# Fixing the order of all engines in the joints into the even and the odd layer, with the norms split into steps between the products

## Chip, cores and metric

One core of one Trainium2 chip. The time is that of the whole program on the device, in microseconds (us), as a median of runs.

## What is computed

Two blocks, one after the other, on 1024 rows of 1024 features. The first is a transformer layer with experts; the second has an even and an odd layer. The places of this change are where the even layer begins (behind the experts' scatter) and where the odd layer begins (behind the even layer's output projection). Both begin with a row norm and a large projection:

```python
def rmsnorm_2(x, g):
    xf = x.astype(jnp.float32)
    y = xf * lax.rsqrt(jnp.mean(xf * xf, axis=-1, keepdims=True) + EPS)
    return (y * g.astype(jnp.float32)).astype(x.dtype)

def even_layer(x, norm_g, w_in, pool_w, pool_scale, ws, bs, w_out):
    h = rmsnorm_2(x, norm_g)
    z = h @ w_in
    ...
    return x + jnp.concatenate([y_a, y_b], axis=-1) @ w_out

def odd_layer(x, norm_g, w_in, conv_w, w_out):
    h = rmsnorm_2(x, norm_g)
    z = h @ w_in
    ...
```

## The kernel before

Rows of x are handled as eight token tiles of 128; tiles t and t + 4 form a pair, so there are four pairs, t = 0 to 3. The projections run as seven products of half-size matrices instead of eight (B11, T2, T1, T3, B21, T4, B22; `unit`, L1212 to L1266), each matmul on a high and a low part of its operands, 12 matmuls a product. They need sums of the halves of the weight and of the normed, transposed x.

`norm_pair` makes those of x for one pair. It squares both tiles on ScalarE (ACT, L230), forms 1/rms with small steps on VectorE (DVE) and one root on ACT (`rstd`, L176 to L182), multiplies the first tile by 1/rms and the norm's row on DVE (L1283) and the second on ACT (L1284) and GpSimd (POOL, L1285), transposes four blocks on TensorE (PE, L1291), and writes seven operands with a high part (cast on ACT, L1297) and a low part (DVE L136 or POOL L134), with differences on DVE (L1302 to L1310). Called with a `high_priority` hint, it is woven by the scheduler into what stands around it. The squares' output that nobody reads (`junk`) takes a buffer of the tag pq, of which there are two, as for the unit's p1, q and r.

`operands` is a generator that loads weight quarters (`raw`), forms the four sums S (L1182, L1183, L1187, L1192) on DVE and splits each operand (`split`: cast L1166 on ACT, low part L134 on POOL). `feed` draws the first seven operands of a stage.

`unit` runs seven products into three banks a, b, c of the tag mm: p1 = B11 is copied by ACT (L1242), q = p1 + T2 on DVE (L1245), r = q + T3 on DVE (L1251), and the results leave through `put` (L1262 copy on ACT, L1264 sum on DVE). T2, T3 and T4 go through the same bank b. With `sub` it does one half of the columns, 256 wide: the first half needs the pairs t = 0 and 1, the second (`sub` = 1) t = 2 and 3. So a stage begins: norms of t0 and t1, half unit 0, norms of t2 and t3, half unit 1, then units 512 wide.

**Joint into the even layer** (`even`, first part). Behind the last expert's scatter into xacc on POOL (L1154) the x tiles are loaded (L1402, queue of SyncE, SP), and the row `nrow` (L1397) after the first four of them. Banks for the transposes: s, o, s, o.

**Joint into the odd layer** (end of `even`). The last pass of `out_sums` multiplies the last slice of the even output projection, into two banks of the tag o, and DVE adds each half of a tile to x (the eviction, L1363), in the order of tiles 0, 4, 1, 5, 2, 6, 3, 7; `then` stores each to x3d (L1457) and calls the norm of t0 after tile 5 and of t1 after tile 7. The tags mm and s have three banks, o has two:

```python
self.banks(es, "secp", {"mm": 3, "s": 3, "o": 2})
...
self.out_sums(A["weo"], self.ye, [((15,), (0, 4, 1, 5, 2, 6, 3, 7), then)], ("o",))
self.feed([A["wo7"][i] for i in range(56)], ("X",) * 3)
self.qk = [self.t("qk", [D]) for _ in range(2)]
self.unit(self.put2(self.qk), None, 0)
norm(2)
norm(3)
self.unit(self.put2(self.qk, 0, 1), None, 1)
```

## Time and profile before

| what | value |
|---|---|
| median of 3 runs | 3397.22 us (3395.42 to 3404.03) |
| profiled execution, own time | 3398.43 us |
| its span, first to last instruction | 3396.6 us |
| mean granted TensorE clock | 0.959 |
| TensorE busy | 3097.2 us, 91% |
| DVE, POOL, ACT busy | 2058.0, 1490.8, 1368.6 us |

Times in the rows below are microseconds from the start of the span. An engine's share of busy time is a mean over stages with different limits; the table by stretches shows it stage by stage, and the timeline of one engine shows what each instruction waited for.

### The profile page before, as it was taken

The page shows a single profiled execution, that of the slowest core. Times are in us where ns is not written, and L with a number is a line of the kernel's source. Part 1 is how long each engine was busy: PE and PEld are TensorE (multiplying, and loading weights), DVE is VectorE, ACT ScalarE, POOL GpSimd, SP SyncE. Part 2 cuts the span into 40 slices and gives each one's busy share as a digit, 9 for nine tenths or more (in the row PEclk, how much of TensorE's full clock was granted, in tenths as well). Part 3 has the DMA queues.
Part 4 walks back from the last instruction along what each step waited for, and adds up shares of the span by engine and source line. Part 5 has one row for each costly group of instructions (what it writes and reads, how often), then busy time and mean ns, then how long its engine had stood idle before and what let it go on. Part 6 is the DMA issues. An engine that isn't in the chain of part 4 may idle for free. (4 is left out here: it accounts for less than half of the span.)

```text
span 3396.6 us, 43830 instructions
## 1 busy us (share of the span) xinstructions
PE 3097.2 (91%) x15797; PEld 2559.2 (75%) x15797; DVE 2058.0 (61%) x3793; ACT 1368.6 (40%) x2489; POOL 1490.8 (44%) x1014
## 2 busy tenths in 40 slices
PE   6898888994999679999998899999999999999998
PEld 4787675773777568887786788888888888877787
DVE  5676677776899864555546555555455455444455
ACT  4445345442787643332312434334334333232312
POOL 2443342322233355556563434334334334566673
PEclk8899898897999889999999999999999999999999
DMA  5233321436999512212441111111111111122242
GB/s 195 69 124 101 116 69 42 136 101 238 331 382 375 163 54 75 69 59 75 153 145 66 37 41 53 44 50 47 48 50 46 49 44 50 53 72 68 100 154 75
DMA packets 139710, 358.38 MB, mean 106 GB/s; under 512 B 16946, under 2 KB 26706, under 8 KB 139492
## 3 DMA queue, kind: packets, MB, share of 16 engines
q1 hardware_dynamic: 134596, 337.75, 29.0%
q0 software_dynamic: 4896, 17.83, 2.1%
q8 instruction: 124, 2.03, 0.2%
q14 instruction: 94, 0.77, 0.1%
HBM read 307.23 MB, written 48.28 MB: 105 GB/s over the span
## 5 line engine op out<-in xcount | busy, mean ns | idle before, releaser
L1234 PE MATMUL ps_mm<-h,hi 128*128 128x512 f32 (+1 forms) x4272 | 1089.9, 394 | 41.0 <-DVE pq L1251 10.9
L1234 PEld LDWEIGHTS ps_mm<-h,hi 128*128 128x128 f32 x4272 | 784.0, 189 | 210.9 <-ACT qk L1262 17.2
L134 POOL TENSOR_TENSOR lo<-S,hi 128x512 fp32r<-128x512 f32 x302 | 402.9, 1337 | 600.1 <-PE ps_mm L1234 411.0
L134 POOL TENSOR_TENSOR lo<-raw,hi 128x512 fp32r<-128x512 f32 (+2 forms) x274 | 416.6, 1526 | 345.5 <-ACT hi L1166 219.0
L1234 PE MATMUL ps_mm<-h,lo 128*128 128x512 f32 (+1 forms) x2136 | 566.0, 388 | 0.0
L1234 PEld LDWEIGHTS ps_mm<-h,lo 128*128 128x128 f32 x2136 | 398.9, 189 | 82.5
L1166 ACT CAST hi<-S 128x512 fp32r<-128x512 f32 x302 | 187.0, 620 | 546.4 <-PE ps_mm L1234 530.8
L1166 ACT CAST hi<-raw 128x512 fp32r<-128x512 f32 x240 | 148.9, 622 | 359.4 <-PE ps_mm L1234 308.8
L148 ACT CAST hi<-raw 128x1024 fp32r<-128x1024 f32 (+1 forms) x222 | 230.4, 1048 | 93.1 <-PE ps_mm L162 64.1
L136 DVE TENSOR_TENSOR lo<-raw,hi 128x1024 fp32r<-128x1024 f32 x188 | 247.8, 1347 | 28.2 <-ACT hi L148 25.0
L1187 DVE TENSOR_TENSOR S<-raw,raw 128x512 f32<-128x512 f32 x76 | 66.6, 876 | 190.6 <-POOL lo L134 189.3
L160 PE MATMUL ps_mm<-hi,hxh 128*128 128x256 f32 (+1 forms) x448 | 132.6, 297 | 9.6 <-ACT hxh L364 5.8
L162 PE MATMUL ps_mm<-hi,hxl 128*128 128x256 f32 (+1 forms) x448 | 131.9, 296 | 1.2 <-POOL hxl L134 1.2
L161 PE MATMUL ps_mm<-lo,hxh 128*128 128x256 f32 (+1 forms) x448 | 131.9, 295 | 0.0
L1153 POOL TENSOR_TENSOR y<-y,g 128x1024 f32<-128x1024 f32 x15 | 41.1, 2738 | 197.0 <-ACT y L1149 197.0
L1183 DVE TENSOR_TENSOR S<-S,raw 128x512 f32<-128x512 f32 x76 | 102.8, 1353 | 37.8 <-POOL lo L134 37.3
L161 PE MATMUL ps_mm<-lo,xT 128*128 128x512 f32 x256 | 105.2, 411 | 13.8 <-DVE lo L136 12.5
L1726 DVE CUSTOM_DVE_ANT_0 P<-ps_s,bias 128x128 f32<-128x128 f32 (+1 forms) x192 | 61.8, 348 | 81.4 <-PE ps_s L1721 80.3
L1264 DVE TENSOR_TENSOR qk<-ps_mm,pq 128x512 f32<-128x512 f32 (+1 forms) x75 | 69.1, 938 | 67.5 <-PE ps_mm L1234 67.2
L134 POOL TENSOR_TENSOR yl<-r,yh 128x1024 fp32r<-128x1024 f32 x28 | 68.3, 2440 | 83.8 <-ACT yh L1335 83.8
L160 PE MATMUL ps_mm<-hi,xT 128*128 128x512 f32 x256 | 103.6, 405 | 0.0
L1335 ACT CAST yh<-r 128x1024 fp32r<-128x1024 f32 x28 | 29.4, 1049 | 181.1 <-PE ps_s L161 167.9
(597 smaller groups left out, 6614.8 us busy)
## 6 DMA issues: line engine op xcount, KB each, us to landing
raw<-in_wexp_dram SPq DMA_DIRECT2D x192, 512.0 KB, 8.3
raw<-in_wo_dram SPq DMA_DIRECT2D x228, 256.0 KB, 2.7
raw<-in_we_dram SPq DMA_DIRECT2D x80, 256.0 KB, 2.8
mraw<-in_wmod_dram SPq DMA_DIRECT2D x64, 256.0 KB, 2.7
r<-ye SPq DMA_DIRECT2D x14, 512.0 KB, 4.6
r<-in_weo_dram SPq DMA_DIRECT2D x14, 512.0 KB
r<-yo SPq DMA_DIRECT2D x14, 512.0 KB, 3.6
r<-in_wo_dram SPq DMA_DIRECT2D x14, 512.0 KB
```

Source lines behind the costliest of these rows:

```text
L134: nc.gpsimd.tensor_sub(lo, raw, hi.bitcast(F32))
L136: nc.vector.tensor_sub(lo, raw, hi.bitcast(F32))
L148: self.nc.scalar.copy(hi, raw)
L160: nc.tensor.matmul(out, l[0], r[0], start=start, stop=False)
L161: nc.tensor.matmul(out, l[0], r[1], start=False, stop=False)
L162: nc.tensor.matmul(out, l[1], r[0], start=False, stop=stop)
L1166: self.nc.scalar.copy(hi, x)
L1183: nc.vector.tensor_sub(s2, s1, a11)
L1187: nc.vector.tensor_sub(s3, a11, a21)
L1234: nc.tensor.matmul(ps, w[a][:, kt * P:(kt + 1) * P], h[b][:, kt, cs], start=start and i == 0, stop=i == 11, skip_group_check=True)
L1264: self.nc.vector.tensor_add(dst, ps, add)
L1726: nc.vector.tensor_tensor_reduce(p, ps, bias[:, n - m:], op0=ALU.add, op1=ALU.max, scale=1.0, scalar=-3e38, accum_out=mx[:, j:j + 1])
```

## The change

In both joints the order of the instructions is fixed as the code writes them (`manual_schedule`), on all five engines in the first, on all but SP in the second. `norm_pair` becomes a generator of two pieces: squares, 1/rms and both multiplies, now both on DVE (L1297 after the change); then transposes (L1304) and operands (L1310 to L1323). In the first half unit, `steps` runs the first piece of t3 behind q (after two products), and the second pieces of t2 and t3 behind the sixth and the seventh product; the first piece of t2 stands ahead of the unit. In the pass's `then`, the first pieces of t0 and t1 come behind tiles 4 and 5, the second ones behind tiles 6 and 7. In `feed` the low parts go to POOL and DVE in turn. `nrow` and the first loads of weights are issued ahead of x. New line numbers: eviction L1377, q L1253, r L1260, puts L1275 and L1277, products L1237, x loads L1414.

```diff
--- before.py
+++ after.py
@@ -1164,7 +1164,7 @@
     def split(self, x, pair=None):
         hi, lo = pair or (self.t("hi", [512], F32R), self.t("lo", [512], F32R))
         self.nc.scalar.copy(hi, x)
-        self.lo_sub(lo, x, hi, "pool")
+        self.lo_sub(lo, x, hi)
         return hi, lo
 
     def operands(self, srcs, pairs):
@@ -1196,9 +1196,11 @@
             a11, a22, a21, a12 = n11, n22, n21, n12
 
     def feed(self, srcs, tiles):
-        pairs = [(x[:, 0], x[:, 1]) for x in (self.spare(t) for t in tiles)]
+        pairs = [(x[:, 0], x[:, 1]) for x in tiles]
         self.ops, self.ready = self.operands(srcs, pairs), []
+        self.lo_engines = ["pool", "dve"]
         self.first = [next(self.ops) for _ in range(7)]
+        self.lo_engines = ["pool"]
 
     def spare(self, tag):
         return self.t(tag, [2, 512], F32R, name="op")
@@ -1209,7 +1211,8 @@
             if o:
                 self.ready.append(o)
 
-    def unit(self, put, hook=None, sub=None):
+    def unit(self, put, hook=None, sub=None, steps={}):
+
 
 
         nc = self.nc
@@ -1236,13 +1239,19 @@
             if sub and done[0] < 5:
                 self.ahead()
 
+        def step():
+            if done[0] in steps:
+                next(steps[done[0]])
+
         a, b, c = (self.pt("mm")[:, :n] for _ in range(3))
         prod(a, "B11")
         p1 = self.t("pq", [n])
         nc.scalar.copy(p1, a)
+        step()
         prod(b, "T2")
         q = self.t("pq", [n])
         nc.vector.tensor_add(q, b, p1)
+        step()
         if hook:
             hook()
         prod(c, "T1")
@@ -1250,12 +1259,16 @@
         r = self.t("pq", [n])
         nc.vector.tensor_add(r, b, q)
         put(1, 1, c, r)
+        step()
         prod(a, "B21", False)
         put(0, 0, a, None)
+        step()
         prod(b, "T4")
         put(1, 0, b, r)
+        step()
         prod(c, "B22", False)
         put(0, 1, c, q)
+        step()
 
     def into(self, dst, ps, add):
         if add is None:
@@ -1280,9 +1293,9 @@
         ss, rs = self.t("ss", [2]), self.t("ss", [2])
         self.norm_rows(xs, rs, ss)
         xn = xs
-        nc.vector.scalar_tensor_tensor(xn[0], xs[0], rs[:, 0:1], row, op0=ALU.mult, op1=ALU.mult)
-        nc.scalar.mul(xn[1], xs[1], rs[:, 1:2])
-        nc.gpsimd.tensor_mul(xn[1], xn[1], row)
+        for i in range(2):
+            nc.vector.scalar_tensor_tensor(xn[i], xs[i], rs[:, i:i + 1], row, op0=ALU.mult, op1=ALU.mult)
+        yield
         ps = {}
         for n, bank in zip(("11", "12", "22", "21"), banks):
             p = ps[n] = self.pt(bank)
@@ -1311,6 +1324,7 @@
         out("T2", t2, "pool")
         out("B21", ps["21"], "dve")
         out("T4", t4, "pool")
+        yield
 
     def out_sums(self, w, y, passes, banks, x=None):
 
@@ -1392,11 +1406,9 @@
             two = lambda tag, n=D: [self.t(tag, [n]) for _ in range(2)]
             tl = two("a", 1040)
             xs = [two("ph"), two("ph")]
-            self.feed([A["we7"][i] for i in range(20)], ("q", "q", "s"))
-            row = self.t("s", [D], name="nrow")
-            nc.sync.dma_start(row, A["en"].to_broadcast([P, D]))
-
-            def norm(t):
+            engines = {e.engine for e in (nc.sync, nc.tensor, nc.scalar, nc.vector, nc.gpsimd)}
+
+            def load(t):
                 x = xs[t] if t < 2 else two("ph")
                 for i in range(2):
                     nc.sync.dma_start(x[i], self.xacc[(t + 4 * i) * P:(t + 4 * i + 1) * P, :])
@@ -1410,16 +1422,21 @@
                         g = self.t("g", [2, 512])
                     return g[:, i % 2]
 
-                with self.tc.high_priority(offset=100):
-                    self.norm_pair(t, x, row, T, ("s", "o", "s", "o"))
-
-            norm(0)
-            norm(1)
-            for a in tl:
-                nc.gpsimd.memset(a[:, 0:16], 0.0)
-            self.unit(self.put2(tl, 16), None, 0)
-            norm(2)
-            norm(3)
+                return self.norm_pair(t, x, row, T, ("s", "o", "s", "o"))
+
+            with self.tc.manual_schedule(engines=engines):
+                op = [self.spare(t) for t in ("q", "q", "s")]
+                row = self.t("s", [D], name="nrow")
+                nc.sync.dma_start(row, A["en"].to_broadcast([P, D]))
+                self.feed([A["we7"][i] for i in range(20)], op)
+                for x in tl:
+                    nc.gpsimd.memset(x[:, 0:16], 0.0)
+                n = [load(0), load(1)]
+                for i in (0, 1, 0, 1):
+                    next(n[i])
+                n += [load(2), load(3)]
+                next(n[2])
+                self.unit(self.put2(tl, 16), None, 0, {2: n[3], 6: n[2], 7: n[3]})
             self.unit(self.put2(tl, 16, 1), None, 1)
             wst, bsb, le = (self.t(k, [4, P], name="w") for k in ("W", "W", "PT"))
             nc.sync.dma_start(wst.rearrange("p a b -> p (a b)"), A["wst"])
@@ -1449,22 +1466,24 @@
                 row = self.t("row", [D])
                 nc.sync.dma_start(row, A["on"].to_broadcast([P, D]))
 
-                def norm(t):
-                    with self.tc.high_priority(offset=100):
-                        self.norm_pair(t, [self.xs[t], self.xs[t + 4]], row, lambda i: self.t("T", [512]), ("s",) * 4)
+                engines = {e.engine for e in (nc.tensor, nc.scalar, nc.vector, nc.gpsimd)}
+                n = [self.norm_pair(t, [self.xs[t], self.xs[t + 4]], row, lambda i: self.t("T", [512]), ("s",) * 4)
+                     for t in range(4)]
 
                 def then(t):
                     nc.sync.dma_start(self.x3d[t * P:(t + 1) * P, :], self.xs[t])
                     self.dump(f"x3_{t}", self.xs[t])
-                    if t in (5, 7):
-                        norm((t - 5) // 2)
-
-                self.out_sums(A["weo"], self.ye, [((15,), (0, 4, 1, 5, 2, 6, 3, 7), then)], ("o",))
-                self.feed([A["wo7"][i] for i in range(56)], ("X",) * 3)
-                self.qk = [self.t("qk", [D]) for _ in range(2)]
-                self.unit(self.put2(self.qk), None, 0)
-                norm(2)
-                norm(3)
+                    if t in (4, 5):
+                        next(n[t - 4])
+                    elif t > 5:
+                        next(n[t - 6])
+
+                with self.tc.manual_schedule(engines=engines):
+                    self.out_sums(A["weo"], self.ye, [((15,), (0, 4, 1, 5, 2, 6, 3, 7), then)], ("o",))
+                    self.feed([A["wo7"][i] for i in range(56)], [self.spare("X") for _ in range(3)])
+                    self.qk = [self.t("qk", [D]) for _ in range(2)]
+                    next(n[2])
+                    self.unit(self.put2(self.qk), None, 0, {2: n[3], 6: n[2], 7: n[3]})
                 self.unit(self.put2(self.qk, 0, 1), None, 1)
 
     def even_group(self, g, tl=None):
```

**DVE, last pass of the output projection.** x_308n are the tiles t0, t4, t1, t5, t2, t6, t3, t7 in this order (n = 0 to 7), ps_o the pass's banks, rst and ss the norm's. Before, from t4's second half on:

```order
L1363 TENSOR_TENSOR x_3081_14435<-x_3081_14435,ps_o_15700 128x512
L1363 TENSOR_TENSOR x_3082_14436<-x_3082_14436,ps_o_15706 128x512
L1363 TENSOR_TENSOR x_3082_14436<-x_3082_14436,ps_o_15711 128x512
L176 TENSOR_SCALAR rst_15734<-ss_15728 128x2
L1363 TENSOR_TENSOR x_3083_14437<-x_3083_14437,ps_o_15717 128x512
L178 RECIPROCAL rst_15734<-rst_15734 128x2
L1363 TENSOR_TENSOR x_3083_14437<-x_3083_14437,ps_o_15722 128x512
L179 TENSOR_TENSOR rst_15734<-rst_15734 128x2
L180 TENSOR_TENSOR rst_15734<-rst_15734 128x2
L1363 TENSOR_TENSOR x_3084_14438<-x_3084_14438,ps_o_15788 128x512
L181 TENSOR_SCALAR rst_15734<-rst_15734 128x2
L1363 TENSOR_TENSOR x_3084_14438<-x_3084_14438,ps_o_15793 128x512
```

and now:

```order
L1377 TENSOR_TENSOR x_3081_14434<-x_3081_14434,ps_o_15701 128x512
L176 TENSOR_SCALAR rst_15713<-ss_15707 128x2
L178 RECIPROCAL rst_15713<-rst_15713 128x2
L179 TENSOR_TENSOR rst_15713<-rst_15713 128x2
L180 TENSOR_TENSOR rst_15713<-rst_15713 128x2
L181 TENSOR_SCALAR rst_15713<-rst_15713 128x2
L182 TENSOR_TENSOR ss_15708<-rst_15713 128x2
L1297 SCALAR_TENSOR_TENSOR x_3080_14433<-x_3080_14433,ss_15708,row_15657 128x1024
L1297 SCALAR_TENSOR_TENSOR x_3081_14434<-x_3081_14434,ss_15708,row_15657 128x1024
L1377 TENSOR_TENSOR x_3082_14435<-x_3082_14435,ps_o_15723 128x512
L1377 TENSOR_TENSOR x_3082_14435<-x_3082_14435,ps_o_15728 128x512
L1377 TENSOR_TENSOR x_3083_14436<-x_3083_14436,ps_o_15734 128x512
```

The norm of t0 stood between the evictions of t1, t5 and t2; now all of it, with two multiplies, stands ahead of t1's.

**DVE, first half unit of the odd layer.** pq are q (L1245, now L1253) and r; S sums of the weights; x_3084 and x_3085 are t2 and t6. Before, behind t1's operands:

```order
L136 TENSOR_TENSOR h_15646<-ps_s_15859,h_15645 128x4x128
L136 TENSOR_TENSOR h_15644<-ps_s_15864,h_15643 128x4x128
L1187 TENSOR_TENSOR S_16235<-raw_15903,raw_15925 128x512
L1245 TENSOR_TENSOR pq_15972<-ps_mm_15944,pq_15958 128x256
L1251 TENSOR_TENSOR pq_15998<-ps_mm_15944,pq_15972 128x256
L1264 TENSOR_TENSOR qk_15942<-ps_mm_15945,pq_15998 128x256
L1264 TENSOR_TENSOR qk_15942<-ps_mm_15944,pq_15998 128x256
L1264 TENSOR_TENSOR qk_15941<-ps_mm_15945,pq_15972 128x256
L176 TENSOR_SCALAR rst_16046<-ss_16040 128x2
L178 RECIPROCAL rst_16046<-rst_16046 128x2
```

and now:

```order
L1182 TENSOR_TENSOR S_16195<-raw_15924,raw_15904 128x512
L1183 TENSOR_TENSOR S_16196<-S_16195,raw_15902 128x512
L1187 TENSOR_TENSOR S_16233<-raw_15902,raw_15924 128x512
L176 TENSOR_SCALAR rst_15948<-ss_15942 128x2
L178 RECIPROCAL rst_15948<-rst_15948 128x2
L179 TENSOR_TENSOR rst_15948<-rst_15948 128x2
L180 TENSOR_TENSOR rst_15948<-rst_15948 128x2
L181 TENSOR_SCALAR rst_15948<-rst_15948 128x2
L182 TENSOR_TENSOR ss_15943<-rst_15948 128x2
L1297 SCALAR_TENSOR_TENSOR x_3084_14437<-x_3084_14437,ss_15943,row_15657 128x1024
L1297 SCALAR_TENSOR_TENSOR x_3085_14438<-x_3085_14438,ss_15943,row_15657 128x1024
L1253 TENSOR_TENSOR pq_15987<-ps_mm_15959,pq_15973 128x256
```

q stood ahead of the norm of t2; now it stands behind it, and the sums of the weights, which were among the evictions, stand behind t1's operands.

**DVE, joint into the even layer.** ph are the x tiles, g and W buffers of the differences of t0 and t1. Before, from the end of t1's 1/rms on:

```order
L181 TENSOR_SCALAR rst_10792<-rst_10792 128x2
L182 TENSOR_TENSOR ss_10787<-rst_10792 128x2
L1283 SCALAR_TENSOR_TENSOR ph_10669<-ph_10669,ss_10727,nrow_10722 128x1024
L1283 SCALAR_TENSOR_TENSOR ph_10671<-ph_10671,ss_10787,nrow_10722 128x1024
L1302 TENSOR_TENSOR g_10763<-g_10763,ps_s_10743 128x512
L1304 TENSOR_TENSOR g_10764<-ps_s_10753,g_10763 128x512
L1306 TENSOR_TENSOR g_10763<-ps_s_10753,g_10763 128x512
L136 TENSOR_TENSOR h_10651<-ps_s_10743,h_10650 128x4x128
L1310 TENSOR_TENSOR g_10764<-ps_o_10758,g_10763 128x512
L1302 TENSOR_TENSOR W_10823<-W_10824,ps_s_10803 128x512
L1304 TENSOR_TENSOR PT_10825<-ps_s_10813,W_10824 128x512
```

and now:

```order
L182 TENSOR_TENSOR ss_10749<-rst_10754 128x2
L1297 SCALAR_TENSOR_TENSOR ph_10671<-ph_10671,ss_10749,nrow_10678 128x1024
L1297 SCALAR_TENSOR_TENSOR ph_10672<-ph_10672,ss_10749,nrow_10678 128x1024
L1315 TENSOR_TENSOR g_10784<-g_10784,ps_s_10764 128x512
L136 TENSOR_TENSOR h_10651<-ps_s_10764,h_10650 128x4x128
L1317 TENSOR_TENSOR g_10785<-ps_s_10774,g_10784 128x512
L1319 TENSOR_TENSOR g_10784<-ps_s_10774,g_10784 128x512
L136 TENSOR_TENSOR h_10655<-ps_s_10774,h_10654 128x4x128
L1323 TENSOR_TENSOR g_10785<-ps_o_10779,g_10784 128x512
L136 TENSOR_TENSOR h_10653<-ps_o_10779,h_10652 128x4x128
L1315 TENSOR_TENSOR W_10825<-W_10826,ps_s_10805 128x512
L136 TENSOR_TENSOR h_10651<-ps_s_10805,h_10650 128x4x128
```

The operands of t0 (g) and t1 (W) were mixed; now t0's seven instructions come first, behind four multiplies.

## Rows read from the trace of the kernel before

**Rows 1.** Page, part 1: busy us, share of the span, instructions.
```profile
PE 3097.2 (91%) x15797; PEld 2559.2 (75%) x15797; DVE 2058.0 (61%) x3793; ACT 1368.6 (40%) x2489; POOL 1490.8 (44%) x1014
```

**Rows 2.** Stretches: bounds; length; busy (instructions) by engine; PEclk; DMA share; GB/s.
```profile
1212.00:1226.00 14.00, 6.30 (x32) 4.95 (x32) 11.07 (x22) 9.98 (x20) 7.60 (x5) 0.76 0.00 1
...
1878.00:1895.00 17.00, 8.31 (x33) 5.97 (x32) 12.56 (x24) 11.29 (x23) 9.68 (x6) 0.61 0.00 0
...
1910.00:1940.00 30.00, 29.32 (x135) 24.13 (x134) 12.79 (x34) 11.85 (x29) 12.38 (x11) 1.00 0.18 56
1940.00:2400.00 460.00, 453.06 (x2336) 383.06 (x2335) 251.00 (x559) 169.50 (x390) 182.64 (x142) 1.00 0.15 47
```

**Rows 3.** Timeline, DVE, last pass: start us, us, engine line operation [idle before <-releaser].
```profile
1837.42 1.38 DVE L1363 TENSOR_TENSOR x<-x,ps_o 128x512 f32<-128x512 f32 x2 [0.37 <-PE ps_o L162]
...
1840.91 0.69 DVE L1363 TENSOR_TENSOR x<-x,ps_o 128x512 f32<-128x512 f32 x1
...
1842.41 1.28 DVE L1283 SCALAR_TENSOR_TENSOR x<-x,ss,row 128x1024 f32<-128x1024 f32 x1
1843.61 1.28 DVE L1363 TENSOR_TENSOR x<-x,ps_o 128x512 f32<-128x512 f32 x2
```

**Rows 4.** Timeline, ACT, joint into the odd layer.
```profile
1837.09 1.06 ACT L230 ACTIVATE junk<-x 128x1024 bf16<-128x1024 f32 x1 [0.60 <-DVE x L1363]
...
1839.55 0.20 ACT L177 ACTIVATE rst<-rst 128x2 f32<-128x2 f32 x1
...
1860.78 0.58 ACT L1301 COPY T<-ps_s 128x512 f32<-128x512 f32 x1 [2.44 <-PE ps_s L1291]
...
1877.19 1.06 ACT L230 ACTIVATE junk<-x 128x1024 bf16<-128x1024 f32 x1 [7.28 <-DVE qk L1264]
```

**Rows 5.** Timeline, DVE, rest of that joint.
```profile
1866.59 0.69 DVE L136 TENSOR_TENSOR h<-ps_s,h 128x512 fp32r<-128x512 f32 x1 [0.24 <-ACT h L1297]
...
1872.24 0.42 DVE L1245 TENSOR_TENSOR pq<-ps_mm,pq 128x256 f32<-128x256 f32 x1 [3.80 <-PE ps_mm L1234]
1874.46 0.42 DVE L1251 TENSOR_TENSOR pq<-ps_mm,pq 128x256 f32<-128x256 f32 x1 [1.79 <-PE ps_mm L1234]
...
1879.55 0.17 DVE L176 TENSOR_SCALAR rst<-ss 128x2 f32<-128x2 f32 x1 [1.02 <-ACT junk L230]
...
1880.98 1.28 DVE L1283 SCALAR_TENSOR_TENSOR x<-x,ss,row 128x1024 f32<-128x1024 f32 x1
```

**Rows 6.** Timeline of that joint: TensorE's first products of both halves, then POOL.
```profile
1863.66 2.58 PE L1234 MATMUL ps_mm<-h,hi 128*128 128x256 f32 x8 [0.40 <-ACT h L1297]
...
1895.09 0.53 PE L1234 MATMUL ps_mm<-h,hi 128*128 128x256 f32 x1 [0.29 <-ACT h L1297]
...
1889.81 4.98 POOL L134 TENSOR_TENSOR h<-T,h 128x512 fp32r<-128x512 f32 x4
```

**Rows 7.** Timeline, DVE, joint into the even layer.
```profile
1167.67 7.59 DVE L1187 TENSOR_TENSOR S<-raw,raw 128x512 f32<-128x512 f32 x1
...
1186.06 6.72 DVE L1283 SCALAR_TENSOR_TENSOR ph<-ph,ss,nrow 128x1024 f32<-128x1024 f32 x2
1192.71 0.68 DVE L1302 TENSOR_TENSOR g<-g,ps_s 128x512 f32<-128x512 f32 x1
...
1201.34 0.69 DVE L136 TENSOR_TENSOR h<-ps_o,h 128x512 fp32r<-128x512 f32 x1 [0.65 <-ACT h L1297]
1205.00 0.42 DVE L1245 TENSOR_TENSOR pq<-ps_mm,pq 128x256 f32<-128x256 f32 x1 [2.97 <-PE ps_mm L1234]
```

**Rows 8.** Timeline of the same joint: POOL, then ACT, then TensorE.
```profile
1186.06 5.65 POOL L1285 TENSOR_TENSOR ph<-ph,nrow 128x1024 f32<-128x1024 f32 x2 [3.44 <-DMA nrow<-in_en_dram]
...
1179.28 1.28 ACT L177 ACT_TABLE_LOAD   x1
...
1197.17 0.39 PE L1234 MATMUL ps_mm<-h,hi 128*128 128x256 f32 x1 [0.58 <-ACT h L1297]
...
1228.24 1.10 PE L1234 MATMUL ps_mm<-h,hi 128*128 128x256 f32 x7 [1.31 <-DVE h L136]
```

## The prediction

> **What bounds the kernel now.** I read the page first: TensorE is busy 91% of the span [rows 1]. The table by stage then shows where it is not. From 1910 us on it works 29.3 of 30 us and 453 of 460 us: there the time is that of its matmuls, and whatever reaches it late earlier on moves everything behind it, one for one, to the end. In the two joints it has holes: 6.3 us of work in 14 (1212 to 1226) and 8.3 in 17 (1878 to 1895) [rows 2]. So I price each joint by how much earlier or later TensorE leaves it. The rows of DVE and ACT in the joints come last, for the change alters what stands behind what on these two.
>
> **Joint into the odd layer: the last pass.** Two ps_o banks let TensorE run two halves ahead of DVE's evictions, no more. Before, these go on while the norm of t0 advances: t1's first half leaves at 1837.42, t2's at 1840.91, and t0's multiply slips in at 1842.41 [rows 3]. Now DVE holds, in this order: t0 and t4, their norm with both multiplies, t1 and t5, the next norm, t2 and t6. Each norm waits for ACT, and the evictions queued behind it wait too.
> First norm: ACT's second square (1837.09) and the table load behind it don't depend on the order, and the root comes at 1839.55 [rows 4]. From L176 to the multiply it is 1.43 us (1879.55 to 1880.98 [rows 5]), of which 0.2 lie ahead of the root: multiply at 1840.8. Two multiplies at 1.20 us each (1842.41 to 1843.61 [rows 3]): t1's first half leaves at 1843.2, **5.8 us late**.
> Then two banks wait filled, 2 x 0.6 us. The other two halves come at TensorE's pace: 1.38 + 0.37 us for two at the full clock [rows 3], at worst double, since the clock sinks where the engine stands (0.61 granted from 1878 to 1895 [rows 2]). So 2.9 to 4.7 us for four halves; I take 4.2, near the slow end, because TensorE has just stood for 5 us. t5 is out at 1847.4; one square is 1.2 (two take 2.4 with their waits, 1877.19 to 1879.55 [rows 4, 5]), the chain 1.4, the multiplies 2.4: t2's first half leaves at 1852.4, **11.5 us late**, and t6 is out at 1856.6.
>
> **First product.** t0's transposes now stand on TensorE behind t6's matmuls, and t0's operands on DVE ahead of t3 and t7. One tile's operands took 6.5 us (copy at 1860.78 [rows 4] to the last subtraction, 1866.59 + 0.69 [rows 5]), transposes ahead of them 0.6 and the wait for the first copy as much (0.58 there): 1864.3. Evictions of t3 and t7, 4.3: 1868.6. t1, again 1.2 + 6.5: 1876.3. The first product was at 1863.66 [rows 6] and comes at 1876.5, **12.8 us late**.
>
> **Weights, then t2 and t3.** The seven first operands were cast and subtracted under the evictions. Now DVE's seven instructions for them (7 x 0.6 us) and POOL's four (4 x 1.24, from four that took 4.98 [rows 6]) come after t1's operands. I take them as one chain, 4.2 + 5.0, and 1.1 for two casts that are waited for: 10.3 us, to 1886.6. Bounds: 5.0 (POOL alone) and 16 (if POOL's and DVE's stalls double each DVE instruction and add the casts). ACT squares t2 behind its last cast: squares and chain 3.8 (1877.19 [rows 4] to 1880.98 [rows 5]), multiplies 2.4: **q at 1892.8**, where it was at 1872.24 [rows 5]. That is the second thing the order does: q stands behind t2's norm, and r behind t3's, whose squares need p1's buffer and so wait for q: 0.4 + 3.8 + 2.4, **r at 1899.4** (before 1874.46 [rows 5]). TensorE's T3 product waits for q and T4 for r, since T2, T3 and T4 use one bank that q and r empty. What is gained: the norms of t2 and t3 are over when T4 runs. Before, their squares began at 1877.19 and the second half unit came 17.9 us later, at 1895.09 [rows 4, 6]. Now from r on: 0.4, T4 2.6 us (as eight matmuls of the first product took at 1863.66 [rows 6]), transposes and copy 1.2, t2's operands 6.5, t3's first operand 2: 1912.1, against 1895.09 17.0 late. I add 0.5 for the three DVE sums of the next operand that stand ahead of t2's norm, one of them behind a raw load: **+17.5 us**. That load also moves behind the eight x3d stores on SP, at no cost: its buffer comes free only with the weights' third difference, after the last store. ACT's scaling and POOL's row multiplication of each tile fall away; what TensorE waited for them is inside the 17.9.
>
> **Joint into the even layer.** SP's x loads stand behind two more weight loads, but all wait for the last scatter anyway; x lands when it did. t0's multiply waited for the row (POOL idle 3.44 us for nrow [rows 8]). Now the row is there and the multiply follows ACT's table load, 1179.28 + 1.28 [rows 8], by 1.5: 1182.1 instead of 1186.06, and two take 2.4 us, not 6.72, as POOL no longer multiplies [rows 7]. That is a lead of 4 to 6 us. But DVE then does t1's norm and multiplies (1.4 + 2.4, some waits) before any operand: 1188.5; t0's operands 6.5: 1195.0; t1's first, 1.8 (copy, difference and cast of 0.6 each): first product 1196.8 against 1197.17 [rows 8]. The lead is spent: before, the operands of both tiles were mixed and took 9.3 us together (1192.71 to 1201.34 + 0.69 [rows 7]), now 13. Then q waits for t2's norm: squares from 1201.9, 3.8 + 2.4: 1208.1 against 1205.00 [rows 7]; r 6.6 later, 1214.7; then as above 0.4 + 2.6 + 1.2 + 6.5 + 2: 1227.4. Before, all but the first matmul of that half unit stood until 1228.24 [rows 8]. **I take 0 us**, bounds -6 (the lead kept) and +7 (r's lateness uncovered).
>
> **Sum.** 3398.43 us (the profiled execution; its span is 3396.6) + 17.5 = 3415.9. That execution lies 1.2 us above the median of the runs, 3397.22; against the median the forecast is **3415 us**. A measurement of this kernel can tell 0.3%, some 10 us.
>
> **POOL and DVE.** Three of the weights' subtractions move from POOL to DVE. The rows: a multiply took 1.28 us alone [rows 3] and two took 6.72 beside POOL; one DVE difference took 7.59 us under a row of POOL subtractions [rows 7]. In my sum the two engines take turns. The Trainium skill, GPSIMD Engine Reference, section Specifications, has POOL's SBUF interfaces shared with VectorE, with contention for DVE instructions that have two SBUF inputs. By that rule these three are exposed as the difference was, and rival (c) is what it would make of the time; the 7.59 agrees.
>
> **Rivals.**
> (a) *The holes close.* The first product comes 12.8 us late as above, but q and r cost TensorE nothing: then each hole shrinks by the norms that move into the unit, 2 x (2.4 + 1.4 + 1.2) = 10 us less the 3 that POOL's part overlapped, 7: 12.8 - 7 - 7, 3396, no change. For it: the holes are large [rows 2]. Against: T3 and T4 need the bank that q and r empty, and nothing stands between. 0.13.
> (b) *Faster.* As (a), and the second norm doesn't hold t2's evictions, so that only the first 5.8 us are lost: 5.8 - 14, 3389. It decides by whether t2's first half leaves before about 1847. Against it: the order of DVE as built. 0.08.
> (c) *POOL starves DVE* in the weights' chain: one stall of 7.59 - 0.68, some 7 us, in the odd joint: 3422. Against: in the new order most of POOL's subtractions wait for a DVE result, so that they can't run in a row. 0.11.
> (d) That the order isn't what the code asks is excluded by the rows of the built order.
>
> **Numbers.** Main case 0.68, (a) 0.13, (b) 0.08, (c) 0.11. Slower by over 0.3% (above 3407.4): the main case but its fastest end, and (c), 0.77. Within: (a) and that end, 0.15. Faster: (b), 0.08. The range takes the main case with the bounds of the pace and of the weights' chain (-1.3 and +0.5 twice, -5 and +6) and with part of the even joint's (-6), and (c): 3402 to 3423; outside lie (a), (b) in 0.2.
>
> **What would show it.** In the last pass TensorE should stand twice for 5 to 6 us, released by L1377, with t1 evicted near 1843 and t2 near 1852. In the odd joint the first product should come near 1876.5, q (L1253) near 1893, r (L1260) near 1899, the second half unit near 1912.5; in the even joint the multiplies near 1182, the first product near 1197, q near 1208, the second half unit near 1228. I am wrong if t2 is evicted before 1847, or if the hole ahead of the second half unit is gone without q and r being late.

## The result: slower, 3418.5 us against 3399.1

The changed kernel takes 3418.46 us (median of four runs, 3414.06 to 3421.71), the kernel before 3399.05 us beside it (3395.42 to 3404.03). The ratio is 1.0059, 95% interval 1.0046 to 1.0071: some 19 us slower, or 0.59%.

**Profile after: where TensorE leaves the joints.** The profiled execution took 3414.06 us, its span is 3412.3. To place the loss I measure each joint on its own clock. The even joint runs from the last expert's last row y on DVE (L1151) to a fixed 512-wide product on TensorE (the sixth of them, the one that waits 0.96 us for r), the odd joint from the first square of its norms on ACT (L230) to the second 512-wide product there. I call these lengths the two marks. Timeline of the kernel before, the rows that bound them (DVE, PE, ACT, PE):

```profile
1165.68 0.75 DVE L1151 SCALAR_TENSOR_TENSOR y<-ps_mm,gate,g 128x512 f32<-128x512 f32 x1 [1.28 <-PE ps_mm L162]
...
1256.66 2.06 PE L1234 MATMUL ps_mm<-h,hi 128*128 128x512 f32 x8 [0.96 <-DVE pq L1251]
...
1835.34 1.06 ACT L230 ACTIVATE junk<-x 128x1024 bf16<-128x1024 f32 x1 [42.57 <-DVE x L1363]
...
1910.32 2.00 PE L1234 MATMUL ps_mm<-h,hi 128*128 128x512 f32 x8
```

The same rows of the kernel after:

```profile
1163.72 0.75 DVE L1151 SCALAR_TENSOR_TENSOR y<-ps_mm,gate,g 128x512 f32<-128x512 f32 x1 [1.12 <-PE ps_mm L162]
...
1255.65 2.08 PE L1237 MATMUL ps_mm<-h,hi 128*128 128x512 f32 x8 [0.96 <-DVE pq L1260]
...
1832.16 1.06 ACT L230 ACTIVATE junk<-x 128x1024 bf16<-128x1024 f32 x1 [42.57 <-DVE x L1377]
...
1925.34 2.00 PE L1237 MATMUL ps_mm<-h,hi 128*128 128x512 f32 x8
```

The even joint's mark goes from 90.98 to 91.93 us (+0.95), the odd joint's from 74.98 to 93.18 (+18.2). Together 19.15, and the medians lie 19.4 apart. What lies ahead of, between and behind the joints differs by -1.96, -2.17 and +0.68 us in these two executions (1163.72 against 1165.68, and so on); that is why the spans differ by only 15.7.

**Profile after: DVE in the odd joint.** Timeline of the kernel after, DVE:

```profile
1837.62 2.48 DVE L1297 SCALAR_TENSOR_TENSOR x<-x,ss,row 128x1024 f32<-128x1024 f32 x2
1840.02 1.28 DVE L1377 TENSOR_TENSOR x<-x,ps_o 128x512 f32<-128x512 f32 x2
...
1847.11 2.48 DVE L1297 SCALAR_TENSOR_TENSOR x<-x,ss,row 128x1024 f32<-128x1024 f32 x2
1849.51 1.28 DVE L1377 TENSOR_TENSOR x<-x,ps_o 128x512 f32<-128x512 f32 x2
...
1861.45 1.28 DVE L1377 TENSOR_TENSOR x<-x,ps_o 128x512 f32<-128x512 f32 x2
...
1888.58 2.48 DVE L1297 SCALAR_TENSOR_TENSOR x<-x,ss,row 128x1024 f32<-128x1024 f32 x2
1890.97 0.42 DVE L1253 TENSOR_TENSOR pq<-ps_mm,pq 128x256 f32<-128x256 f32 x1
...
1895.22 2.48 DVE L1297 SCALAR_TENSOR_TENSOR x<-x,ss,row 128x1024 f32<-128x1024 f32 x2
1897.61 0.42 DVE L1260 TENSOR_TENSOR pq<-ps_mm,pq 128x256 f32<-128x256 f32 x1
```

Each pair of evictions (L1377) stands right behind a pair of multiplies (L1297); the third pair stands behind t0's operands. Then q and r stand behind the multiplies of t2 and of t3. TensorE of the same stretch answers to each of these:

```profile
1840.75 0.79 PE L160 MATMUL ps_o<-hi,hi 128*128 128x512 f32 x1 [5.84 <-DVE x L1377]
...
1850.24 0.80 PE L160 MATMUL ps_o<-hi,hi 128*128 128x512 f32 x1 [4.00 <-DVE x L1377]
...
1862.19 0.79 PE L160 MATMUL ps_o<-hi,hi 128*128 128x512 f32 x1 [5.28 <-DVE x L1377]
...
1874.60 2.08 PE L1237 MATMUL ps_mm<-h,hi 128*128 128x256 f32 x8 [6.45 <-ACT hi L1166]
...
1891.44 2.07 PE L1237 MATMUL ps_mm<-h,hi 128*128 128x256 f32 x8 [9.06 <-DVE pq L1253]
...
1898.09 1.70 PE L1237 MATMUL ps_mm<-h,op 128*128 128x256 f32 x12 [1.15 <-DVE pq L1260]
...
1909.81 2.58 PE L1237 MATMUL ps_mm<-h,hi 128*128 128x256 f32 x8
```

Three waits for evictions (15.1 us), one for the first cast of the weights (6.45), one for q (9.06) and one for r (1.15). The table by stage of the kernel after shows the same; its columns are those of [rows 2]:

```profile
1212.00:1226.00 14.00, 8.05 (x56) 7.64 (x54) 7.88 (x13) 5.28 (x10) 4.11 (x4) 0.85 0.00 0
...
1857.00:1863.00 6.00, 0.81 (x2) 0.72 (x3) 4.32 (x7) 2.83 (x5) 4.81 (x4) 0.75 0.01 1
...
1878.00:1895.00 17.00, 7.94 (x42) 7.47 (x42) 12.76 (x22) 8.12 (x17) 4.15 (x3) 0.70 0.26 79
1910.00:1940.00 30.00, 29.86 (x164) 26.61 (x164) 14.06 (x31) 9.84 (x18) 17.19 (x14) 0.92 0.17 51
1940.00:2400.00 460.00, 452.38 (x2304) 381.23 (x2303) 249.91 (x560) 174.14 (x406) 184.51 (x144) 1.00 0.15 48
```

From 1910 on TensorE is as full as before [rows 2]; 1878 to 1895 still holds 9 us of idle time; from 1857 to 1863, a stretch of the evictions now, it does almost nothing.

**Profile after: the even joint.** Timeline of the kernel after, DVE and then PE:

```profile
1181.50 2.48 DVE L1297 SCALAR_TENSOR_TENSOR ph<-ph,ss,nrow 128x1024 f32<-128x1024 f32 x2
...
1207.15 0.42 DVE L1253 TENSOR_TENSOR pq<-ps_mm,pq 128x256 f32<-128x256 f32 x1
...
1213.79 0.42 DVE L1260 TENSOR_TENSOR pq<-ps_mm,pq 128x256 f32<-128x256 f32 x1
```

```profile
1196.08 2.59 PE L1237 MATMUL ps_mm<-h,hi 128*128 128x256 f32 x8 [0.44 <-ACT h L1310]
...
1227.57 2.59 PE L1237 MATMUL ps_mm<-h,hi 128*128 128x256 f32 x8 [0.51 <-ACT h L1310]
```

Counted from y, the multiplies come 2.6 us earlier than before (17.8 against 20.4, 1186.06 [rows 7] less 1165.68), the first product 0.9 later (32.4 against 31.5), and the second half unit 1.3 later.

### The profile page after: what moved, and what is told of

It is laid out like the page before. It is cut to its first block, busy times and chain, and to the rows that moved or that the text cites. A ratio compares the mean times of both kernels' runs of the same rounds, so it can differ in the third digit from the quotient of the medians.

```text
span 3412.3 us, 43818 instructions
## 1 busy us (share of the span) xinstructions
PE 3104.5 (91%) x15797; PEld 2568.0 (75%) x15797; DVE 2055.1 (60%) x3807; ACT 1363.2 (40%) x2481; POOL 1461.9 (43%) x1000
## 4 chain that ended last, share of the span: by engine, by line
PE 69%; DVE 13%; DMA 5%; issue 4%; ACT 4%; POOL 3%; SPq 0%; DVEq 0%; ACTq 0%; POOLq 0%
PE ps_mm L1237 40%; PE ps_mm L161 3%; PE ps_mm L162 3%; PE ps_mm L160 3%; DVE lo L136 2%; PE ps_o L1813 2%; DMA raw<-in_wexp_dram 2%; PE ps_s L1740 2%; DMA mraw<-in_wmod_dram 2%; PE ps_s L160 1%; PE ps_s L161 1%; PE ps_s L162 1%; PE ps_O L956 1%; DVE macc L328 1%; PE ps_tr L949 1%
## 5 line engine op out<-in xcount | busy, mean ns | idle before, releaser
L1237 PE MATMUL ps_mm<-h,hi 128*128 128x512 f32 (+1 forms) x4272 | 1095.6, 396 | 54.1 <-DVE pq L1253 11.3
L1237 PEld LDWEIGHTS ps_mm<-h,hi 128*128 128x128 f32 x4272 | 789.3, 191 | 224.4 <-ACT qk L1275 17.2
L1237 PE MATMUL ps_mm<-h,lo 128*128 128x512 f32 (+1 forms) x2136 | 568.2, 389 | 0.4 <-POOL lo L134 0.4
L1237 PEld LDWEIGHTS ps_mm<-h,lo 128*128 128x128 f32 x2136 | 400.8, 190 | 83.0 <-POOL lo L134 0.7
L1187 DVE TENSOR_TENSOR S<-raw,raw 128x512 f32<-128x512 f32 x76 | 58.0, 763 | 190.0 <-POOL lo L134 188.8
L1277 DVE TENSOR_TENSOR qk<-ps_mm,pq 128x512 f32<-128x512 f32 (+1 forms) x75 | 69.1, 940 | 65.4 <-PE ps_mm L1237 65.1
```

Source lines behind the costliest of these rows:

```text
L1237: nc.tensor.matmul(ps, w[a][:, kt * P:(kt + 1) * P], h[b][:, kt, cs], start=start and i == 0, stop=i == 11, skip_group_check=True)
L1277: self.nc.vector.tensor_add(dst, ps, add)
```

## The experiments

All compare with the kernel before, on the same chip. Theory A, unless a run says otherwise, is the prediction's: the written order sets the loss, through the evictions and through what stands behind what on DVE and ACT. The rivals are told with each run. Each mark comes from one profiled execution. Where kernels share a joint's code and its order is written, the marks of that joint lie within 0.7 us (even joint 91.2 to 91.9). Where the scheduler sets the order they can lie further apart: the odd joint has the same lines in runs 7, 8 and 10, run 8 has them in another order, and the marks are 69.7, 66.5 and 69.8. Marks of all runs, in us:

| kernel | even joint | odd joint | ratio to before (95%) |
|---|---|---|---|
| before | 91.0 | 75.0 | |
| changed | 91.9 | 93.2 | 1.0059 (1.0046 to 1.0071) |
| 1 even joint alone | 91.3 | 74.7 | 1.0007 (0.9998 to 1.0017) |
| 2 odd joint alone | 90.5 | 93.3 | 1.0052 (1.0035 to 1.0069) |
| 3 evictions free | 91.4 | 86.7 | 1.0037 (1.0023 to 1.0051) |
| 4 q ahead of the norms | 93.4 | 93.7 | 1.0054 (1.0037 to 1.0070) |
| 5 odd joint scheduled | 91.2 | 74.4 | 1.0015 (1.0005 to 1.0024) |
| 6 multiplies on DVE | 88.2 | 76.6 | 0.9992 (0.9983 to 1.0002) |
| 7 squares in W, raw; row ahead | 80.0 | 69.7 | 0.9946 (0.9930 to 0.9963) |
| 8 squares in PT, raw; row ahead | 80.0 | 66.5 | 0.9935 (0.9919 to 0.9952) |
| 9 row ahead alone | 87.5 | 74.8 | 1.0003 (0.9993 to 1.0012) |
| 10 squares in PT, raw alone | 82.0 | 69.8 | 0.9942 (0.9925 to 0.9959) |
| 11 changed, squares in PT, raw | 87.8 | 91.3 | 1.0040 (1.0026 to 1.0054) |
| 12 weights between, evictions free | 90.9 | 84.6 | 1.0035 (1.0021 to 1.0049) |

### 1 and 2: one joint at a time

Run 1 is the change in the even joint, with the odd joint's code of before; run 2 the reverse. Of run 1, against the changed kernel:

```diff
-                    if t in (4, 5):
-                        next(n[t - 4])
-                    elif t > 5:
-                        next(n[t - 6])
+                    if t in (5, 7):
+                        norm((t - 5) // 2)
...
-                with self.tc.manual_schedule(engines=engines):
...
-                    next(n[2])
-                    self.unit(self.put2(self.qk), None, 0, {2: n[3], 6: n[2], 7: n[3]})
+                self.unit(self.put2(self.qk), None, 0)
+                norm(2)
+                norm(3)
```

> The change in the joint into the even layer alone; the joint into the odd layer as before. Theory A (the loss comes from the odd joint, the even one gives and takes about the same): 3399 to 3401 us, within 0.1% of the kernel before; from the last expert's y to the first product of the third unit about 94 to 95 us (93.8 before). Theory B (q and r behind the norms cost the same in both joints): some 7 to 9 us more than before. Theory C (the even joint keeps the 4 to 6 us by which its multiplies come earlier): 3393 to 3395 us.

Measured: 3399.07 us, ratio 1.0007.

> The change in the joint into the odd layer alone; the joint into the even layer as before. Theory A: 3399 + 18 = 3417 us, the whole of the change. Theory B: some 3408, half of it. Theory C: more than the whole change, 3422.

Measured: 3414.03 us, ratio 1.0052, 17 us over the kernel before beside it (3397.06). So the loss lies in the odd joint, and the even joint is worth next to nothing either way, as its mark says.

### 3: the evictions free of the norms

The order stays written, but the norms' first pieces come one tile later in the pass, and the second ones behind the whole pass, so that the evictions of two more tiles go ahead of each:

```diff
-                    if t in (4, 5):
-                        next(n[t - 4])
-                    elif t > 5:
-                        next(n[t - 6])
+                    for k in {5: (0,), 6: (1,), 7: (0, 1)}.get(t, ()):
+                        next(n[k])
```

> The changed kernel, but in the last pass the norm of t0 comes behind tile 5 and that of t1 behind tile 6, and both tiles' operands behind tile 7, so that no eviction stands behind a norm that has to wait. Theory A (a chain on DVE and ACT: stalls of the evictions, weights behind the operands, the tiles' operands one after the other; all add up): the last pass ends some 12 us earlier, but the operands and the weights still follow in a row, so 5 to 6 us of the 19 come back: about 3413 us. Theory D (the eviction stalls are the loss): the first product comes 11 to 13 us earlier and the time falls to 3405 to 3407.

Measured: 3408.93 us (3403.92 to 3415.30), ratio 1.0037. The time lies between the two forecasts and can't decide between them. The mark is 86.7, 6.5 us earlier than in the changed kernel, and the first product 6.3 earlier, not the 11 to 13 of theory D. t1's first half leaves 2.1 us after the first square, as before, and t2's at 9.0 (5.6 before, 17.4 changed). But the first product still waits, for the same row (timeline of run 3, PE, then ACT):

```profile
1870.33 2.08 PE L1237 MATMUL ps_mm<-h,hi 128*128 128x256 f32 x8 [5.63 <-ACT hi L1166]
```

```profile
1869.66 0.62 ACT L1166 CAST hi<-raw 128x512 fp32r<-128x512 f32 x1
```

The cast of the weights that it waits for needs none of x; it stands on ACT behind the last operand of t1.

### 4: q and r ahead of the norms

In both joints t2's first piece comes behind q and t3's behind the sixth product, so that q waits for no norm, and r for t2's in place of t3's:

```diff
-                    next(n[2])
-                    self.unit(self.put2(self.qk), None, 0, {2: n[3], 6: n[2], 7: n[3]})
+                    self.unit(self.put2(self.qk), None, 0, {2: (n[2],), 6: (n[3],), 7: (n[2], n[3])})
```

> The changed kernel, but in both joints t2's norm stands behind q (not ahead of it) and t3's behind the first result of T4 (not ahead of r), with the operands of t2 and t3 behind the seventh product. Theory B (q and r behind the norms are a loss of their own): T3 starts some 7 us earlier after the first product and the second half unit with it, 6 to 7 us less in each joint: about 3405 us. Theory A (the norms of t2 and t3 and their operands are a chain on DVE and ACT that has to be gone through either way): q and T3 come 6 to 7 us earlier, but the second half unit's first product moves by less than 1 us in either joint: 3417 to 3419 us.

Measured: 3415.92 us, ratio 1.0054. Timeline of run 4, DVE, then ACT, then PE (its first square is at 1838.42):

```profile
1891.31 0.42 DVE L1253 TENSOR_TENSOR pq<-ps_mm,pq 128x256 f32<-128x256 f32 x1
...
1895.56 2.48 DVE L1297 SCALAR_TENSOR_TENSOR x<-x,ss,row 128x1024 f32<-128x1024 f32 x2
1897.95 0.42 DVE L1260 TENSOR_TENSOR pq<-ps_mm,pq 128x256 f32<-128x256 f32 x1
...
1905.70 2.48 DVE L1297 SCALAR_TENSOR_TENSOR x<-x,ss,row 128x1024 f32<-128x1024 f32 x2
...
1908.43 0.68 DVE L1315 TENSOR_TENSOR T<-T,ps_s 128x512 f32<-128x512 f32 x1
```

```profile
1901.91 1.06 ACT L230 ACTIVATE junk<-x 128x1024 bf16<-128x1024 f32 x1 [6.59 <-DVE qk L1277]
```

```profile
1898.42 5.49 PE L1237 MATMUL ps_mm<-h,op 128*128 128x256 f32 x24 [3.51 <-DVE pq L1260]
...
1916.86 2.59 PE L1237 MATMUL ps_mm<-h,hi 128*128 128x256 f32 x8
```

q and r come 5.9 us earlier after the first square than in the changed kernel (52.9 and 59.5 against 58.8 and 65.5), but the second half unit does not: 78.4 against 77.7. t2's multiplies stand where they stood (57.1 against 56.4), t3's 4.2 later. So an earlier q is worth nothing by itself in this order. What q and r cost the changed kernel this run does not show, for it puts other waits in: r now stands behind t2's multiplies and holds TensorE 3.51 us, t3's squares wait 6.59 us for a buffer of pq, and t2's operands (L1315) stand on DVE behind t3's multiplies.

### 5: the scheduler's order back

The changed kernel with the odd joint's manual order taken off. All other content stays: both multiplies on DVE, the low parts on POOL and DVE in turn, the steps' places in the program.

```diff
-                with self.tc.manual_schedule(engines=engines):
+                if True:
```

> The changed kernel with the odd joint's manual order taken off and nothing else: its steps stand at the same places in the program and its multiplies and half of its lo parts stay on DVE, but the scheduler sets the order of the engines there again; the even joint stays as changed. Theory A (the 18 us of the odd joint come from the written order, which puts the evictions of t1 and t2 behind the additions of the expert's rows and the norms of t2 and t3 behind the weights' feed): first product about 28 us after the first square, as before (before 28.3, changed 42.4), the 512-wide products' mark at 73 to 77 (before 75.0, changed 93.2), 3396 to 3403 us. Rival D (the content does it: two more multiplies and half of the feed's subtractions on DVE): first product at 38 to 43, mark at 85 to 93, 3409 to 3418 us.

Measured: 3401.37 us, ratio 1.0015; mark 74.4, first product 31.9 us after the first square and not 28. In the odd joint the order is the loss and the content is not: its mark is back at that of before, 18.7 us earlier. The 4 us by which the time still lies over before are in neither mark. In this run the weights' first cast is at 12.2 us after the first square, among the evictions (timeline of run 5, ACT; first square 1838.93); in the changed kernel it is at 41.8, in run 3 at 35.5. t2's squares come at 18.8, in the changed kernel at 52.

```profile
1851.12 0.62 ACT L1166 CAST hi<-raw 128x512 fp32r<-128x512 f32 x1
```

### 6: the multiplies on DVE, without the order

```diff
-        nc.scalar.mul(xn[1], xs[1], rs[:, 1:2])
-        nc.gpsimd.tensor_mul(xn[1], xn[1], row)
+        nc.vector.scalar_tensor_tensor(xn[1], xs[1], rs[:, 1:2], row, op0=ALU.mult, op1=ALU.mult)
```

> The kernel before, with both multiplies of every norm on DVE as one instruction each, in place of one on DVE and a pair on ACT and POOL; the scheduler keeps the order. Theory A (where POOL's multiply and DVE's ran beside each other in the even joint both took 6.7 us in place of 2.5 for two alone, so there the split path costs some 5 us; in the odd joint the chain goes over ACT and the change of engine is worth 1 us either way): even joint's mark 3 to 6 us earlier (91.0 before), odd joint's within 2 us of 75.0, 3392 to 3398 us. Rival (DVE has no room: each unit's q, r and put wait behind two multiplies): even joint's mark the same or later, odd joint's 2 to 5 later, 3399 to 3405 us.

Measured: 3396.19 us; the interval takes in 1. In the marks the even joint gains 2.8 us, a little less than was expected, and the odd one loses 1.6, less than the 3.2 by which the scheduler's order alone moved a mark (runs 7 and 8). This part of the change, alone, is about neutral.

### 7 to 10: why the holes were there

The prediction took the holes of before as given. The row that ends the idle time ahead of t2's squares names their cause: 7.28 us <-DVE qk L1264 [rows 4]. The squares' output is thrown away, but it takes a buffer of the tag pq, which p1, q and r go through too; the squares of t2 wait until the first puts free one. Runs 7 and 8 are the kernel before, no order written, with another tag for that buffer:

```diff
-            self.feed([A["we7"][i] for i in range(20)], ("q", "q", "s"))
+            self.jtag = "PT"
+            tiles = [self.spare(t) for t in ("q", "q", "s")]
             row = self.t("s", [D], name="nrow")
             nc.sync.dma_start(row, A["en"].to_broadcast([P, D]))
+            self.feed([A["we7"][i] for i in range(20)], tiles)
...
             self.unit(self.put2(tl, 16, 1), None, 1)
+            self.jtag = "pq"
...
+                self.jtag = "raw"
                 row = self.t("row", [D])
...
                 self.unit(self.put2(self.qk, 0, 1), None, 1)
+                self.jtag = "pq"
```

This is run 8; run 7 has `"W"` for `"PT"`. Run 9 is the lines on the row and the feed alone, run 10 those with `jtag` alone.

> The kernel before with two small edits: the even joint's row is loaded ahead of x (as in the change), and the squares' throw-away output takes a buffer of another tag (W in the even joint, raw in the odd one) in place of one of the tag pq, which p1, q and r rotate through. Theory E (the holes that the change went for come from that shared tag: the squares of t2 wait 7.3 us in the odd joint and 3.8 in the even one until r and the first puts free a buffer): squares of t2 start before q, even joint's mark 6 to 10 us earlier than 91.0, odd joint's 3 to 6 earlier than 75.0, 3383 to 3391 us. Rival (the squares start early but their norm's transposes and operands then wait for banks, buffers or DVE, and the product waits as long): marks within 2 us of before, 3395 to 3400 us.

Measured: 3379.36 us (3378.22 to 3386.65), ratio 0.9946, a little better than expected; marks 80.0 and 69.7.

> As the run before it, but the even joint's throw-away output in a buffer of the tag PT and not W. Theory E: as with W within 2 us, 3382 to 3391 us, so that it is the release from pq that counts and not which tag takes it. Rival (the tag that takes it hands the wait on to its own users, the transposes' evictions): the even joint's mark 3 us or more apart from that of the run with W.

Measured: 3375.44 us (3373.94 to 3376.26), ratio 0.9935, 95% interval 0.9919 to 0.9952. That is below the range given, and 3.9 us under run 7 where within 2 was expected. The even joint's mark is that of run 7, so the tag there isn't the cause; the odd one's is 3.2 us less, where the two runs have the same lines and only the scheduler's order differs. This is the fastest kernel of the study, 22 us under before and 43 under the change. Runs 9 and 10 take its two edits apart.

> The kernel before with the even joint's row loaded ahead of the first x and nothing else. Theory E (the gain of the two runs before comes from the squares' buffer): even joint's mark 0 to 3 us earlier than 91.0, odd joint's unchanged at 75, 3394 to 3398 us. Rival (the row's early arrival is most of the even joint's 11 us): mark 6 us or more earlier, 3386 to 3391 us.

Measured: 3398.83 us, ratio 1.0003. The mark is 3.5 us earlier, just past the range given; the time doesn't show it.

> The kernel before with the squares' throw-away output in another tag's buffer (PT in the even joint, raw in the odd one) and the row loaded where it was. Theory E: even joint's mark 8 to 11 us earlier than 91.0, odd joint's 4 to 9 earlier than 75.0, 3376 to 3385 us. Rival as in the run before it: even joint's mark within 5 us of 91.0, 3386 to 3393 us.

Measured: 3377.64 us (3375.12 to 3380.45), ratio 0.9942; marks 82.0 and 69.8. Nearly all of run 8's gain is the buffer. Timeline of run 10, ACT, the first square of the joint and the first ones of t2 and of t3, then PE, the first product and the mark:

```profile
1821.09 1.06 ACT L230 ACTIVATE junk<-x 128x1024 bf16<-128x1024 f32 x1 [42.56 <-DVE x L1363]
...
1842.12 1.06 ACT L230 ACTIVATE junk<-x 128x1024 bf16<-128x1024 f32 x1
...
1851.32 1.07 ACT L230 ACTIVATE junk<-x 128x1024 bf16<-128x1024 f32 x1
```

```profile
1857.12 0.58 PE L1234 MATMUL ps_mm<-h,hi 128*128 128x256 f32 x1 [0.40 <-ACT h L1297]
...
1890.90 2.00 PE L1234 MATMUL ps_mm<-h,hi 128*128 128x512 f32 x8
```

t2's squares come 21.0 us after the first square; before it was 41.9. The first product comes 7.7 us *later* than before (36.0 against 28.3), probably since DVE and ACT now do t2's norm among the other work, and yet the mark is 5.2 earlier. Early squares of t2 are not enough by themselves: run 5 has them at 18.8 us, with t3's waiting 4.44 us for q to free a buffer of pq, and its mark is that of before.

One thing stays open here. Run 10 gains 20.7 us by its medians, but its marks only 14.1. The stretch between the joints is 573.9 us in its profile, 578.7 in that of before, 573.9 in that of run 8 too, and from 575.3 to 579.8 in those of the other runs; no run edits it. What shortens it in these two stays open.

### 11: the buffer in the changed kernel

The changed kernel with the lines of run 10 on `jtag`, the order as written.

> The changed kernel with the squares' throw-away output in the same other tags (PT, raw) and the order kept as written. Theory A (in the changed kernel no square waits for a buffer of pq as long as the written order lets ACT come to it late, so the order and not the buffer sets the odd joint's time): odd joint's mark 0 to 5 us earlier than 93.2, 3411 to 3419 us. Rival (the shared buffer is what holds the changed kernel too, and the order costs little once it is gone): mark under 82, 3398 to 3407 us.

Measured: 3410.68 us, ratio 1.0040, just under the range given. The odd mark gains only 1.9 us (91.3): under the written order ACT comes to t2's squares at 1884.31 without waiting for a buffer, since they stand behind the weights' casts. The even one gains 4.1: there t3's squares waited 3.62 us for q to free p1's buffer, with r behind them, and now don't. The order holds the odd joint, with or without the buffer.

### 12: the weights between t1's operands

Run 3's order, with the seven first operands of the weights drawn one by one between the operands of t1 (`b` is a piece of t1's norm, `f` one operand, `c` t2's first piece):

```diff
+                    g["f"] = self.feed([A["wo7"][i] for i in range(56)], [self.spare("X") for _ in range(3)])
...
+                    self.play('a a a a a a a a a b b f b f b f b f b f b f b f b c c', g)
```

> The changed kernel with the evictions free as in the third run, and with the seven first operands of the weights drawn one by one between the seven operands of t1 in place of behind them all; t2's norm still follows both, and the rest of the order stands. Theory A (DVE and ACT have all of this work to do between the last eviction and t2's norm, so its sum and not its sequence counts, and only the waits inside each chain can be filled): odd joint's mark 2 to 5 us earlier than the third run's 86.7, 3403 to 3408 us. Rival G (the weights' place behind t1 is the rest of the loss, since the first product waits for their first cast): mark at 74 to 79, 3396 to 3402 us.

Measured: 3410.08 us, ratio 1.0035, over the expected 3403 to 3408, and not to be told from run 3. The first product comes 4.4 us earlier than in run 3 (31.7 after the first square), the mark only 2.1 (84.6). Rival G falls: the weights' place behind t1 is not the rest of the loss. Theory A's reading is that DVE and ACT have t0's, t1's and the weights' work to do before t2's norm, whatever its sequence, and that run 5 gains by beginning it during the evictions. This is argued from the rows: a written order with the weights ahead of the last evictions was not tried.

## Why the prediction was right

The forecast was 3415 us with 3402 to 3423, 17.5 us over before; measured were 3418.5, 19.4 over, and 18.2 of them in the odd joint, which was to carry all. Its steps, with the clock of the changed kernel moved by 3.18 us so that the first square of the odd joint falls on that of before:

| odd joint | before | predicted | measured |
|---|---|---|---|
| t1's first half evicted | 1837.4 | 1843.2 | 1843.2 |
| t2's first half evicted | 1840.9 | 1852.4 | 1852.7 |
| first product | 1863.7 | 1876.5 | 1877.8 |
| q | 1872.2 | 1892.8 | 1894.2 |
| r | 1874.5 | 1899.4 | 1900.8 |
| second half unit | 1895.1 | 1912.1 | 1913.0 |
| mark, against before | | +17.5 | +18.2 |

- **The last pass** was right to 0.3 us: the multiplies wait for ACT's root, the evictions behind them, TensorE behind these (three times, 5.84, 4.00 and 5.28 us; the third, behind t0's operands, was in the sum but not among its signs). The slow pace that the sum took for the halves behind the wait is there too: TensorE had 1.00 of its clock up to 1834.90, stood 5.84 us, and had 0.50 (its 1.2 GHz level) from 1840.75 to 1846.00, with 0.63 us a matmul and not 0.39; before, the clock was 1.00 from 1833 to 1843. Run 3 takes back 8.4 of the 11.8 us by which t2 was late, and 6.5 of the 18.2 us of the mark.
- **The first product** is 1.3 us late, and not for the reason given: the sum has it wait for t1's operands, the row for the first cast of the weights, which stands behind them on ACT (6.45 us). A tile's operands also took 7.3 to 7.4 us (from the copy at 1854.20 to 1861.54, from 1866.86 to 1874.24), and not 6.5.
- **The weights' chain** was taken as 10.3 us. From the end of t1's operands (1873.55 + 0.69) to t2's squares (1884.31) it is 10.1. The size is right. POOL's 5.0 us in it don't follow DVE's 4.2 but lie in DVE's four sums, which took 1.64 to 1.78 us each and not 0.6 (below).
- **q and r as "the second thing the order does"** is not shown as a cause. The waits are there (9.06 us for q, 1.15 for r), each step came within 1.4 us, and the sum went the right way since it followed the norms of t2 and t3 to the second half unit. But in run 4 q and r come 6 us earlier and the second half unit no earlier, with new waits in their place. That what counts is the norms' place behind the weights, and that q only stands behind them too, is the likelier reading; run 5, where t2's squares come at 18.8 us and not at 52, fits it, and no written order tested it. So some 12 of the 18.2 us come from the order, but from which part of it stays open.
- **The even joint** was taken as 0; its mark measures +0.95, run 1 alone 0.3, and 1.0007 in time. The steps, moved by 1.96 us to before's y: multiplies 1183.5 (1182.1 predicted), first product 1198.0 (1196.8), q 1209.1 (1208.1), r 1215.8 (1214.7), second half unit 1229.5 (1227.4). All are 1 to 2 us late, the last the most.
- **Rival (c)**, POOL starving DVE, happened, four times in the weights' chain and by 1 us each, inside the chain's 10.1 and not as 7 us on top. It met the four sums; the subtractions moved to DVE took 0.68 to 0.69 us. Run 5 keeps this content, and its odd mark is that of before.
- **Rivals (a) and (b)** needed the holes to close. From 1878 to 1895 TensorE is still idle for 9 us. (b) also needed t2's first half out before 1847; it left at 1852.7.
- **What it left out**: it priced the holes without asking for their cause. The row with 7.28 us was among its own [rows 4]. Runs 7 to 10 show that a buffer's tag, with no order written at all, gives 21 us.

## What to carry to other kernels

An order written by hand also fixes what waits behind each wait: before writing one, list for every instruction that waits what stands behind it on the same engine and was ready; here these were bank evictions and weight casts that needed nothing of the norms. Before moving work to fill a hole, read what released the first instruction after it: if it is a buffer's last reader, another tag for that buffer may do more than an order, as it did here. The first product of a stage is no measure of it: in run 10 it is later and the stage ends earlier, in run 12 it is 4.4 us earlier and the stage gains 2.1.

## What the runs showed of the hardware

A 128x512 sum of two SBUF operands takes DVE 0.68 us alone. Begun while POOL works on two SBUF operands, it ended 0.54 to 0.55 us after POOL's instruction did. Timeline of the kernel after, POOL and then DVE, weights' chain of the odd joint:

```profile
1874.11 1.28 POOL L134 TENSOR_TENSOR h<-T,h 128x512 fp32r<-128x512 f32 x1 [0.67 <-ACT h L1310]
1875.35 1.72 POOL L134 TENSOR_TENSOR lo<-raw,hi 128x512 fp32r<-128x512 f32 x1
1878.86 1.27 POOL L134 TENSOR_TENSOR lo<-S,hi 128x512 fp32r<-128x512 f32 x1 [1.80 <-ACT hi L1166]
1881.93 1.27 POOL L134 TENSOR_TENSOR op<-raw,op 128x512 fp32r<-128x512 f32 x1 [1.80 <-ACT op L1166]
```

```profile
1874.15 1.78 DVE L1182 TENSOR_TENSOR S<-raw,raw 128x512 f32<-128x512 f32 x1
1875.97 1.64 DVE L1183 TENSOR_TENSOR S<-S,raw 128x512 f32<-128x512 f32 x1
...
1878.91 1.77 DVE L1187 TENSOR_TENSOR S<-raw,raw 128x512 f32<-128x512 f32 x1
...
1881.98 1.77 DVE L1192 TENSOR_TENSOR S<-raw,S 128x512 f32<-128x512 f32 x1
1883.67 0.68 DVE L136 TENSOR_TENSOR op<-raw,op 128x512 fp32r<-128x512 f32 x1
```

POOL's ends are 1875.39, 1877.07, 1880.13 and 1883.20; DVE's 1875.93, 1877.61, 1880.68 and 1883.75. The last row, which meets no POOL instruction, takes 0.68. Instructions of DVE that read one operand from PSUM, as L1323 at 1872.21 (0.68 us), ran at their own pace beside POOL (busy from 1870.90 to 1873.43). How many POOL instructions DVE waits for differs. Above it waits for one: the sum of 1874.15 ends at 1875.93, with POOL's next instruction, begun at 1875.35, under way, and that one took 1.72 us and not 1.28. The difference of 7.59 us in the kernel before [rows 7] waited for five: it ends at 1175.26, 0.55 after the last of five subtractions of POOL, and DVE did not come in between them. In the profile these five begin 1.22 us apart and last 1.82 to 1.85 each, so that each begins before the one ahead of it has ended; what else sets the two cases apart stays open. The Trainium skill, GPSIMD Engine Reference, section Specifications, names DVE instructions with two SBUF inputs among those that contend with POOL, and its Trainium Architecture — The Big Picture, section What this means for kernel authors, calls the port an exclusive lock and no split of bandwidth; the rows agree.
